# Token dispatch on one core: output tiles of 16 tokens with 64 KB rows, two buffers, and every third product on ScalarE

## The chip, the core and the metric

The kernel runs on one core of a Trainium2 chip. The metric is the device time of one execution in microseconds (us); lower is better. The tensor engine has nothing to do here. The work is done by the DMA engines, which move data between HBM and the on-chip memory (SBUF), and by VectorE (DVE in the profile) and ScalarE (ACT), which multiply. SyncE (SP) multiplies nothing; it issues DMAs.

## The reference

Every token has 512 values and two weights. The output holds each token twice, once scaled by each weight. The expert indices are an input that the result does not depend on.

```python
batch, seq, hidden, n_experts = 16, 1024, 512, 8
k = 2
x_expanded = x[:, :, np.newaxis, :].repeat(k, axis=2)
weights = expert_weights[..., np.newaxis]
return (x_expanded * weights).astype(np.float32)
```

With 16,384 tokens in float32, 33.6 MB are read and 67.1 MB are written.

## The kernel before

The tokens are cut into eight tiles of 2048. In each tile, a partition (one of 128) holds 16 consecutive tokens. Its part of the input is then one contiguous row of 16 x 512 x 4 bytes, 32 KB, and its part of the output is one contiguous row of 64 KB.

**Loads.** `load(i)` takes one input tile of 4 MB into one of two buffers of `x_pool` (line 76). It is issued on ScalarE's queue, so it stands in program order between ScalarE's products. The first two loads are issued ahead of the loop, and `load(i + 2)` at the end of turn `i` (line 109). The eight small weight loads (line 55, 16 KB each) are issued on SP's queue at the start.

**Products.** A tile needs 32 products: 16 tokens times two weights, each over 128 partitions x 512 values. The product of the first weight (`kk == 0`) runs on VectorE (line 97), that of the second (`kk == 1`) on ScalarE (line 91). The number `c` counts the products over the whole kernel: token number times two, plus `kk`.

**Output tiles.** An output tile holds `TO = 8` tokens, so a row of it is 32 KB per partition, and each tile of tokens fills two. `o_pool` has four such buffers. When the eighth token is done, SP issues the store of 4 MB (line 105). It waits there for both engines' products. There are 16 stores.

**What sets the order.** The three queues (SP, ScalarE, VectorE) run in program order, each on its own. A scheduler places the instructions and adds the waits: a product waits for its input tile, for the weights, and for the store that last used its output buffer; a load waits for the products that last read its input buffer. In the built order of the kernel before, each `load(i + 2)` stands behind the first ScalarE product of tile `i + 1`. Every DMA is spread over the same sixteen DMA engines: 128 rows, eight rows to an engine.

Of the kernel before, what the change touches and what calls it, by code (L numbers as in the profile page):

```python
# [1 line left out]

# [4 lines left out]


@with_exitstack
def kernel(  # L10
    ctx: ExitStack,
    tc: tile.TileContext,
    x: bass.AP,
    expert_indices: bass.AP,
    expert_weights: bass.AP,
    out: bass.AP,
):
    nc = tc.nc

    batch, seq, hidden = x.shape  # L20
    k = expert_weights.shape[-1]
    P = nc.NUM_PARTITIONS
    ntok = batch * seq
    assert ntok % P == 0
    A_TOTAL = ntok // P

    f32 = mybir.dt.float32
    row = k * hidden
    TX = 16
    TO = 8  # L30


    groups = [[16], [16], [16], [16], [16], [16], [16], [16]]
    assert sum(sum(g) for g in groups) == A_TOTAL

    xf = x.rearrange("b s h -> (b s) h")
    of = out.rearrange("b s k h -> (b s) (k h)")
    wf = expert_weights.rearrange("b s k -> (b s) k")

    w_pool = ctx.enter_context(tc.tile_pool(name="w_pool", bufs=1))  # L40
    x_pool = ctx.enter_context(tc.tile_pool(name="x_pool", bufs=2))
    o_pool = ctx.enter_context(tc.tile_pool(name="o_pool", bufs=4))

    w_tile = w_pool.tile([P, A_TOTAL * k], f32)

    def rows(of_all, done, T):
        return of_all[done * P : (done + T) * P, :].rearrange(
            "(p a) n -> p (a n)", a=T
        )

    weights = []
    for group in groups:
        weights.append((sum(n for _, n in weights), sum(group)))
    for at, T in weights:
        nc.sync.dma_start(out=w_tile[:, at * k : (at + T) * k], in_=rows(wf, at, T))

    tiles = []
    done = 0
    for group in groups:
        T = sum(group)  # L60
        a0 = 0
        for n in group:
            tiles.append((done, T, a0, n))
            a0 += n
        done += T

    loaded = []

    def load(i):
        if i >= len(tiles):  # L70
            return
        done, T, a0, n = tiles[i]
        x_tile = x_pool.tile([P, TX * hidden], f32)
        cols = rows(xf, done, T)[:, a0 * hidden : (a0 + n) * hidden]
        for lo, hi in [(0, P)]:
            nc.scalar.dma_start(out=x_tile[lo:hi, : n * hidden], in_=cols[lo:hi, :])  # L76
        loaded.append(x_tile)

    for i in range(2):
        load(i)  # L80
    for i, (done, T, a0, n) in enumerate(tiles):
        x_tile = loaded[i]
        outr = rows(of, done, T)
        for t in range(n):
            if t % TO == 0:
                o_tile = o_pool.tile([P, TO * row], f32)
            for kk in range(k):
                c = (done + a0 + t) * k + kk
                o = t % TO * row + kk * hidden
                if kk == 1:  # L90
                    nc.scalar.mul(  # L91
                        out=o_tile[:, o : o + hidden],
                        in_=x_tile[:, t * hidden : (t + 1) * hidden],
                        mul=w_tile[:, c : c + 1],
                    )
                    continue
                nc.vector.tensor_scalar(  # L97
                    out=o_tile[:, o : o + hidden],
                    in0=x_tile[:, t * hidden : (t + 1) * hidden],
                    scalar1=w_tile[:, c : c + 1],  # L100
                    scalar2=None,
                    op0=mybir.AluOpType.mult,
                )
            if (t + 1) % TO == 0:
                nc.sync.dma_start(
                    out=outr[:, (a0 + t + 1 - TO) * row : (a0 + t + 1) * row],
                    in_=o_tile,
                )
        load(i + 2)

# [1 line left out]
_INS = ['x', 'expert_indices', 'expert_weights']  # L112
_OUTS = [((16, 1024, 2, 512), 'float32')]


# [23 lines left out]
```

## Time and profile before

| | |
|---|---|
| median of 11 runs | 240.22 us (240.01 to 241.35) |
| the profiled execution, its own time | 241.35 us |
| its span, first to last instruction | 239.6 us |
| VectorE busy | 51.9 us, 128 products of 480 ns |
| ScalarE busy | 81.3 us, 128 products of 708 ns and a table load |
| moved by DMA | 100.81 MB, mean 421 GB/s |
| DMA issues | 16 stores of 4096 KB, 8 loads of 4096 KB, 8 weight loads of 16 KB |

The profile shows one execution. A row for a group of instructions gives how often it ran, how long it was busy and how long one took. The mean length of one product is longer than the distance from one to the next, since they overlap at their ends: 16 products take 6.42 us on VectorE and 9.91 us on ScalarE. The row of tenths for DMA says how busy the sixteen engines were in each of 40 equal slices, and the row under it how much they moved. The queue named q1 carries what SP issues, q10 what ScalarE issues. Beside the page, the trace keeps a record for every DMA packet: when it started, how long it took, its size and its queue. One packet here is one row of a DMA.

### The profile page before, as it was taken

How to read it: one execution, taken by the hardware profiler on the slowest of the kernel's cores; microseconds unless marked ns; L12 is line 12 of the kernel's file. 1: busy time of each engine (PE TensorE's matmuls, PEld its weight loads, DVE VectorE, ACT ScalarE, POOL GpSimd, SP SyncE). 2: the span in 40 equal slices, each digit the busy share in tenths (PEclk: the TensorE clock that was granted, in tenths of full speed). 3: DMA queues.
4: the chain of work that ended last, by engine and by line, in shares of the span. 5: the costliest groups of instructions: out<-in, count | busy, mean ns of one | idle time of the engine just before them, and what ended most of it. 6: DMA issues, size and time to landing. Idle time of an engine off the chain costs nothing.

```text
span 239.6 us, 384 instructions
## 1 busy us (share of the span) xinstructions
DVE 51.9 (22%) x128; ACT 81.3 (34%) x129; POOL 0.2 (0%) x4
## 2 busy tenths in 40 slices
DVE  0073820055005005050140502204041235000000
ACT  0179880085306108070160803507043266200000
POOL 0000000000000000000000000000000000000000
DMA  6999999999999999999999999999999999999995
GB/s 265 434 439 365 439 438 438 438 427 438 432 416 438 424 372 432 432 438 438 438 427 427 438 427 427 432 427 432 438 432 438 438 438 438 432 432 432 438 438 224
DMA packets 4610, 100.81 MB, mean 421 GB/s; under 512 B 1536, under 2 KB 1536, under 8 KB 1536
## 3 DMA queue, kind: packets, MB, share of 16 engines
q1 hardware_dynamic: 3456, 67.24, 65.3%
q10 hardware_dynamic: 1152, 33.55, 33.3%
q14 instruction: 2, 0.02, 0.0%
HBM read 33.69 MB, written 67.11 MB: 421 GB/s over the span
## 4 chain that ended last, share of the span: by engine, by line
DMA 60%; another core or an unknown queue 12%; ACT 12%; ACTq 1%; issue 0%
DMA out_dram<-o_tile 40%; DMA x_tile<-in_x_dram 18%; ACT o_tile L91 12%; DMA w_tile<-in_expert_weights_dram 2%; ACTq L76 0%; ACTq L134 0%; ACTq L91 0%
## 5 line engine op out<-in xcount | busy, mean ns | idle before, releaser
L91 ACT ACTIVATE o_tile<-x_tile,w_tile 128x512 f32<-128x512 f32 x128 | 80.0, 708 | 118.3 <-DMA out_dram<-o_tile 96.4
L97 DVE TENSOR_SCALAR o_tile<-x_tile,w_tile 128x512 f32<-128x512 f32 x128 | 51.9, 480 | 151.5 <-DMA out_dram<-o_tile 115.9
L91 ACT ACT_TABLE_LOAD x1 | 1.3, 1283 | 5.4 <-DMA w_tile<-in_expert_weights_dram 5.4
L123 POOL MEMSET const-bfloat16-1.0<- 128x1 bf16 x1 | 0.1, 102 | 0.0
L123 POOL MEMSET const-uint8-127<- 128x1 uint8 x1 | 0.1, 102 | 0.0
L123 POOL MEMSET const-float32-0.0<- 128x1 f32 x1 | 0.1, 99 | 0.2 <-issue 0.2
L123 POOL MEMSET const-float32-1.0<- 128x1 f32 x1 | 0.1, 99 | 0.0
## 6 DMA issues: line engine op xcount, KB each, us to landing
out_dram<-o_tile SPq DMA_DIRECT2D x16, 4096.0 KB, 48.4
x_tile<-in_x_dram ACTq DMA_DIRECT2D x8, 4096.0 KB, 23.1
w_tile<-in_expert_weights_dram SPq DMA_DIRECT2D x8, 16.0 KB, 21.7
```

Source lines behind the costliest of these rows:

```text
L91: nc.scalar.mul(out=o_tile[:, o : o + hidden], in_=x_tile[:, t * hidden : (t + 1) * hidden], mul=w_tile[:, c : c + 1],)
L97: nc.vector.tensor_scalar(out=o_tile[:, o : o + hidden], in0=x_tile[:, t * hidden : (t + 1) * hidden], scalar1=w_tile[:, c : c + 1], scala ...
L123: nc = _bacc.Bacc("TRN2", target_bir_lowering=False, num_devices=1)
```

## The change

An output tile now holds 16 tokens: one per tile of tokens, with rows of 64 KB, in two buffers instead of four of half the size. The memory taken is the same. Tile 0 is stored in two pieces, after 8 and after 16 tokens; each of the other seven is stored by one DMA of 8 MB. The products are split by `c % 3`: where it is 2 the product runs on ScalarE (85 in all), otherwise on VectorE (171).

```diff
-    TO = 8
+    TO = 16
...
-    o_pool = ctx.enter_context(tc.tile_pool(name="o_pool", bufs=4))
+    o_pool = ctx.enter_context(tc.tile_pool(name="o_pool", bufs=2))
...
-                if kk == 1:
+                if c % 3 == 2:
                     nc.scalar.mul(
...
-            if (t + 1) % TO == 0:
+
+            n_out = TO // 2 if i == 0 else TO
+            if (t + 1) % n_out == 0:
+                at = t + 1 - n_out
                 nc.sync.dma_start(
-                    out=outr[:, (a0 + t + 1 - TO) * row : (a0 + t + 1) * row],
-                    in_=o_tile,
+                    out=outr[:, (a0 + at) * row : (a0 + t + 1) * row],
+                    in_=o_tile[:, at % TO * row : (at % TO + n_out) * row],
                 )
```

The order of the built instructions changes with it. SP issues nine stores instead of sixteen. On ScalarE, `load(2)` still stands behind the first product of tile 1, but each later `load(i + 2)` now stands behind the last product of tile `i`, ahead of the first product of tile `i + 1`. A product of tile `i` waits for the whole store of tile `i - 2`; the first products of tile 2 wait for both pieces of tile 0.

## The prediction

> **What bounds the kernel now.** I read the page from the top: first the busy shares of the engines, then the DMA row of the 40 slices and the queues, and last who waits for whom.
>
> ```profile
> span 239.6 us, 384 instructions
> DVE 51.9 (22%) x128; ACT 81.3 (34%) x129; POOL 0.2 (0%) x4
> ...
> DMA  6999999999999999999999999999999999999995
> GB/s 265 434 439 365 439 438 438 438 427 438 432 416 438 424 372 432 432 438 438 438 427 427 438 427 427 432 427 432 438 432 438 438 438 438 432 432 432 438 438 224
> ...
> q1 hardware_dynamic: 3456, 67.24, 65.3%
> q10 hardware_dynamic: 1152, 33.55, 33.3%
> ```
>
> No compute engine is busy for more than 34% of the span, and the DMA row is 9 everywhere but in the first and last slice. q1 (stores, and the small weight loads) and q10 (input loads) together take 98.6% of sixteen engines' span. So the sixteen DMA engines are the bound, and only two things can move the time: how long their packets take, and how long they have nothing to do. The stretches say where the missing 1.4% lies (columns: stretch, length, busy us and count of DVE, ACT and POOL, clock, DMA share, GB/s):
>
> ```profile
> 0.00:2.00 2.00, 0.00 (x0) 0.00 (x0) 0.20 (x4) 1.00 0.34 88
> 2.00:20.00 18.00, 6.35 (x16) 7.64 (x12) 0.00 (x0) 1.00 1.00 428
> 20.00:24.00 4.00, 0.07 (x1) 3.55 (x6) 0.00 (x0) 1.00 0.93 283
> 24.00:54.00 30.00, 9.69 (x24) 14.93 (x24) 0.00 (x0) 1.00 1.01 437
> ...
> 84.00:88.00 4.00, 0.00 (x0) 0.00 (x0) 0.00 (x0) 1.00 0.97 336
> 88.00:150.00 62.00, 15.01 (x37) 22.11 (x36) 0.00 (x0) 1.00 1.01 434
> 150.00:210.00 60.00, 14.30 (x36) 22.96 (x37) 0.00 (x0) 1.00 1.00 431
> 210.00:236.00 26.00, 0.00 (x0) 0.00 (x0) 0.00 (x0) 1.00 1.02 439
> ```
>
> Between 24 us and 236 us the rate is 430 to 439 GB/s whether loads and stores mix (24 to 54) or stores run alone (210 to 236), with one dip at 84 to 88. The engines' waits then read differently from what their size suggests:
>
> ```profile
> DVE o_tile L97 <- DMA out_dram<-o_tile: 115.9, 11, 13.8
> ACT o_tile L91 <- DMA out_dram<-o_tile: 96.4, 11, 12.0
> DVE o_tile L97 <- DMA x_tile<-in_x_dram: 35.5, 3, 17.1
> ```
>
> They are slack: VectorE and ScalarE wait for buffers while the DMA engines never stop.
>
> The packet records of the same trace give the budget of one DMA engine. It moves 192 packets of 32 KB (64 of loads, 128 of stores). 2915 of the 3072 last 1213 ns: 192 x 1.213 = 232.9 us. Packets that last longer add 2.1 us per engine: 0.4 in the first 6 us, 0.7 at 20 to 24 us, 0.9 at 83 to 89 us. The 128 B packets of the weights add 0.8 and the 4 B packets that signal completion 0.3. First packet at 1.8 us, last end at 238.4 us, 1.2 us to the end of the span. Idle time of an engine inside 4 to 236 us: none.
>
> **The change part by part.** *Longer rows.* 14 stores of 4 MB become 7 of 8 MB, each with 128 rows of 64 KB; the two pieces of tile 0 keep 32 KB rows. Per engine 7 x 16 = 112 packets of 32 KB become 7 x 8 = 56 of 64 KB. The trace has no 64 KB packet, so I take the line through those that it has: 128 B in 13 ns and 32768 B in 1213 ns give 0.03676 ns per byte and 8.3 ns that do not scale; an 8192 B instruction packet would then take 309.5 ns, and the records show 309. So 64 KB takes 2418 ns against 2 x 1213 = 2426, and the change saves 56 x 8.3 = 0.46 us. Bounds: if a row were moved as two pieces, nothing is saved; on the other side a longer row could run slower per byte for a reason that no packet here shows, and 1% of 2.42 us over 56 packets is 1.36 us. I take 0.46, since three sizes lie on one line.
>
> [...]
>
> *Completion packets.* Seven stores fewer, one 4 B packet of 9 ns each on every engine: 0.06 us. The seven issues of 332 ns that go from SP's queue were behind waits of up to 16 us and save nothing.
>
> *Every third product on ScalarE.* A product takes 6.42 / 16 = 0.401 us on VectorE and 9.91 / 16 = 0.62 us on ScalarE, end to end. Tile by tile it was 16 and 16 (6.4 and 9.9 us); now 21 or 22 on VectorE (8.8 us) and 10 or 11 on ScalarE (6.8 us). A whole tile is ready 1.1 us sooner. Nothing waits for that, except perhaps the first store: its 16 products were 8 x 0.62 = 5.0 us after 13.65 and are 11 x 0.401 = 4.4 us now, so it is issued near 18.1 instead of 18.68. The second load's packets occupy the engines until about 23 us either way. Zero.
>
> *Two buffers of 16 tokens.* A product of tile i may now start only when the whole store of tile i-2 has landed (for tile 2: both pieces), where half of it was enough. Behind that wait stands all of tile i, and SP's store of it. The cover is the store of tile i-1, already queued: 8 x 2.418 = 19.3 us if it has the engines to itself, 29.0 us with a load between its packets. Under it must go the landing (1.2 us or so from the end of the span), 8.8 us of products, 0.35 us of issue and 1.1 us to the first packet (0.72 to 1.8 us at the start): 11.4 us. Slack 7.9 us at the least, near the end, where no load runs. Early on it is larger still: tile 1 is ready at 24.83 + 21 x 0.401 = 33.3 us, and the two pieces of tile 0 keep the engines busy to 23.1 + 19.4 = 42.5 us or longer. Zero.
>
> *The two pieces of tile 0.* Piece one is queued about 5 us before the second load's packets end, piece two near 22.5 us. One whole 16-token store would be queued at 22.5 and start at 23.6, just behind the end of the loads; the split keeps that gap closed. Zero against before, which also stored 8 tokens first.
>
> *Loads that move on ScalarE's queue.* Before, load i+2 for i of 1 and more stood behind the first product of tile i+1, which waited for a buffer: load 3 was issued at 48.45 us, load 4 at 73.78. The built order of the changed kernel puts it right behind tile i's products, so load 3 goes out when VectorE has finished tile 1, near 33.3 us. ScalarE ends tile 1 near 24.83 + 11 x 0.62 = 31.7 and waits 1.6 us there, ahead only of products that wait for stores until after 50 us. Loads then queue behind one another with no pause between them. With packets taken in turn, a load gets a third of the time while 64 KB stores run: 8 x (1.213 + 2.418) = 29.0 us, the same as the work of one tile, and it has about two such periods from issue to use.
>
> [...] The records show turns of one row: from 136 to 152 us 96 store and 114 load packets start, in every 2 us some of each. [...]
>
> **Sum.** -0.46 - 0.06 = -0.52 us. The profiled execution of before took 241.35 us (span 239.6, 1.75 around it), so its like would take 240.83. It is among the slowest of the eleven runs; their median is 240.22, and the 0.9 us dip at 84 to 88 us is about what sets it apart. Against the median: 239.70 us.
>
> **The rivals.** *Nothing saved* (0.10): the 64 KB row is moved in two pieces, or its fixed part overlaps its neighbour. Only the completion packets are left: 240.16. For it: nobody sees the fixed part outside of packet lengths. Against it: packets follow each other without idle time, so length is cost.
>
> *The long row is dearer* (0.13), the case that ends slower. The place is every packet of the seven large stores; it decides at 2.426 us a packet, above which the change loses. At +24 ns (1%) it costs 1.34 us, less 0.06: 241.5; at half that, 240.85. For it: nothing of this size has run here. Against it: 8 KB and 32 KB cost the same per byte.
>
> *The store queue runs dry* (0.03): the wait for a whole 16-token buffer takes the place of the one for half. It decides where 11.4 us of landing, products and issue exceed the 19.3 us of the store before; each us above that costs 1 us in each of up to six tiles. If the products had a fifth more time it would still not happen. 242 if it did.
>
> *The dip goes too* (0.04): the slow read packets at 84 to 88 us (2.5 us for the longest) belong to where a load stood. Loads now stand elsewhere; if the median run has 0.6 us of it, the time is 239.1.
>
> **How the numbers follow.** 0.2% is 0.48 us, about what a measurement of this kernel can tell from no change. The main case (0.70) lies at 239.70, its own range 239.2 to 240.1; about 0.54 of it falls beyond 0.48 us and 0.16 within, for the fixed part may be 4.7 ns. Faster: 0.54 + 0.04 = 0.58. Same: 0.16 + 0.10 = 0.26. Slower: 0.13 + 0.03 = 0.16. The range from 239.0 to 241.0 takes in the main case, nothing saved, and the dearer row up to about 0.6%.
>
> **What would show it.** Right: q1 with 56 x 16 + 7 x 16 = 1008 packets fewer, 2448; the share of the two queues still above 98%; stretches from 24 to 236 us at 430 to 439 GB/s; load 3 issued at about 33 us and load 4 at about 63 (16 store and 9 load packets from 23.1 us, landing near 54, and 8.8 of products); VectorE waiting for stores about once a tile, longer each time. Wrong: 64 KB packets longer than 2.426 us (GB/s under 430 while stores run alone), a slice below 9 in the DMA row between the first and the last, VectorE waiting while the DMA share falls, or q1 at some 3344 packets (rows in two pieces).

## The result, and the profile after

The changed kernel takes 244.0 us (median of 13 runs, 240.83 to 245.93) against 240.13 us for the kernel before (50 runs, 239.81 to 241.45). It is slower: the ratio is 1.0087, with a 95% interval from 1.0065 to 1.0110. The ratio, worth 2.1 us, lies below that of the medians (1.016, or 3.9 us) because it leaves out runs more than 1.5% above the fastest of the same kernel, and the changed kernel has four of them. The runs of the changed kernel are spread over 5 us; those of the kernel before stay within 1.7.

The profile is of an execution of 245.2 us, 1.2 us above the median, so it shows more of the loss than a typical run; the second profile of this kernel (246.09 us, below) does too, and no execution of it near 241 us was profiled. First the page, to be held against the same rows of before: span, busy time, the DMA rows in 40 slices, the queues, and the DMA issues (name, queue, count, KB each, median us to landing).

```profile
span 243.3 us, 364 instructions
DVE 68.4 (28%) x171; ACT 54.2 (22%) x86; POOL 0.2 (0%) x4
...
DMA  6999999999999999998999999999999998989891
GB/s 267 433 433 355 431 431 431 431 436 512 389 463 399 442 404 458 409 475 377 463 420 409 474 366 409 393 431 480 409 420 469 393 496 366 496 366 506 356 431 43
...
q1 hardware_dynamic: 2448, 67.24, 64.3%
q10 hardware_dynamic: 1152, 33.55, 33.1%
...
x_tile<-in_x_dram ACTq DMA_DIRECT2D x8, 4096.0 KB, 34.3
out_dram<-o_tile SPq DMA_DIRECT2D x2, 4096.0 KB, 28.7
...
out_dram<-o_tile SPq DMA_DIRECT2D x7, 51.7
```

q1 holds 2448 packets, so each 64 KB row is one packet. The two queues fill 97.4% of the longer span. Four slices before the last show an 8 in the DMA row, but no engine idles there: the page counts a packet in the slice where it starts, and packets are now twice as long. Summed from the start and end of each packet, the sixteen engines are busy all the time in these four slices, and from 4 to 236 us but for 0.5 us in all of single engines at 146 to 173 us. (A slice's GB/s swings more than before for the same reason.) The issues of loads 3 and 4 (start, length, queue), first before, then after, and what VectorE waited for after (us in total, times, longest):

```profile
48.45 0.33 ACTq L76 DMA_DIRECT2D x_tile<-in_x_dram  x1
73.78 0.33 ACTq L76 DMA_DIRECT2D x_tile<-in_x_dram  x1
```
```profile
32.31 0.36 ACTq L76 DMA_DIRECT2D x_tile<-in_x_dram  x1
67.91 0.36 ACTq L76 DMA_DIRECT2D x_tile<-in_x_dram  x1
...
DVE o_tile L97 <- DMA out_dram<-o_tile: 128.9, 6, 27.2
DVE o_tile L97 <- DMA x_tile<-in_x_dram: 15.0, 2, 13.2
```

The stretches say where the time is (stretch, length, busy us and count of DVE, ACT and POOL, clock, DMA share, GB/s; a packet counts where it starts):

```profile
54.00:76.00 22.00, 8.40 (x21) 6.84 (x11) 0.00 (x0) 1.00 1.02 441
76.00:84.00 8.00, 0.00 (x0) 0.00 (x0) 0.00 (x0) 1.00 1.02 438
84.00:88.00 4.00, 0.00 (x0) 0.00 (x0) 0.00 (x0) 1.00 0.91 377
88.00:150.00 62.00, 17.20 (x43) 13.08 (x21) 0.00 (x0) 1.00 1.00 423
...
236.00:238.00 2.00, 0.00 (x0) 0.00 (x0) 0.00 (x0) 1.00 0.68 295
238.00:240.00 2.00, 0.00 (x0) 0.00 (x0) 0.00 (x0) 1.00 0.23 98
240.00:242.00 2.00, 0.00 (x0) 0.00 (x0) 0.00 (x0) 1.00 0.00 0
```

Two things are new. From 88 to 150 us the rate is 423 GB/s instead of 434 (62 x 11 / 434 = 1.6 us), though the DMA engines are busy but for 0.4 us of single ones. And the end is long: a share of 0.23 in two microseconds is 7.4 engine-microseconds, three packets of 2.418 us. Three engines work on after the other thirteen have finished.

The records of the packets show who they are. A record doesn't name its engine, but each packet starts within a few ns of the end of the one before it on its engine, so the records join into sixteen chains of 136 large packets each. "Stretched" is the time by which large packets last longer than 8.3 ns + 0.03676 ns per byte, as a mean over the engines.

| kernel profiled | last packet of each engine ends at (us) | stretched, us per engine |
|---|---|---|
| before | 236.8 to 238.4 | 2.1 |
| before, a second execution (240.2 us) | 236.2 to 237.2 | 1.5 |
| changed | seven at 236.6 to 237.0, six at 238.8 to 239.3, three at 241.4 to 242.1 | 3.55 |

Every engine has the same 72 store and 64 load packets. Where packets of several engines end together, a chain can be joined in more than one way; the ends and the mean don't depend on that, the sum of one chain does. With this reserve, the early ones lost about 2 us in stretched packets, most of it in the first 30 us as before, and the last about 6 to 7. The last end sets the span: 242.1 + 1.2 = 243.3 us. Nine in ten of the 64 KB packets take 2418 ns to the nanosecond, and the stretched ones up to 3033.

### The profile page after: what moved, and what is told of

It is laid out like the page before. It is cut to its first block, busy times and chain, and to the rows that moved or that the text cites. A ratio compares the mean times of both kernels' runs of the same rounds, so it can differ in the third digit from the quotient of the medians.

```text
span 243.3 us, 364 instructions
## 1 busy us (share of the span) xinstructions
DVE 68.4 (28%) x171; ACT 54.2 (22%) x86; POOL 0.2 (0%) x4
## 3 DMA queue, kind: packets, MB, share of 16 engines
q1 hardware_dynamic: 2448, 67.24, 64.3%
## 4 chain that ended last, share of the span: by engine, by line
DMA 58%; another core or an unknown queue 15%; DVE 11%; ACT 2%; issue 1%; DVEq 0%; SPq 0%; ACTq 0%
DMA x_tile<-in_x_dram 37%; DMA out_dram<-o_tile 18%; DVE o_tile L97 11%; DMA w_tile<-in_expert_weights_dram 2%; ACT o_tile L91 2%; DVEq L137 0%; DVEq L97 0%; SPq L108 0%; ACTq L76 0%
## 5 line engine op out<-in xcount | busy, mean ns | idle before, releaser
L97 DVE TENSOR_SCALAR o_tile<-x_tile,w_tile 128x512 f32<-128x512 f32 x171 | 68.4, 480 | 143.9 <-DMA out_dram<-o_tile 128.9
L91 ACT ACTIVATE o_tile<-x_tile,w_tile 128x512 f32<-128x512 f32 x85 | 52.9, 708 | 150.3 <-DMA out_dram<-o_tile 140.2
```

The costliest lines, as they stand in the source:

```text
L91: nc.scalar.mul(out=o_tile[:, o : o + hidden], in_=x_tile[:, t * hidden : (t + 1) * hidden], mul=w_tile[:, c : c + 1],)
L97: nc.vector.tensor_scalar(out=o_tile[:, o : o + hidden], in0=x_tile[:, t * hidden : (t + 1) * hidden], scalar1=w_tile[:, c : c + 1], scala ...
```

## The experiments

Two theories stood at first. Theory 1: 64 KB packets, while loads share the engines, make single engines lose time. Theory 2: the two whole-tile buffers, and the loads that leave a tile earlier, cost the time.

**32 KB rows in the changed kernel** (rows32, and again beside the changed kernel).

```diff
-                nc.sync.dma_start(
-                    out=outr[:, (a0 + at) * row : (a0 + t + 1) * row],
-                    in_=o_tile[:, at % TO * row : (at % TO + n_out) * row],
-                )
+                for lo in range(at, t + 1, TO // 2):
+                    nc.sync.dma_start(
+                        out=outr[:, (a0 + lo) * row : (a0 + lo + TO // 2) * row],
+                        in_=o_tile[:, lo % TO * row : (lo % TO + TO // 2) * row],
+                    )
```

> The changed kernel, but each of the seven whole tiles is stored by two DMAs with 32 KB rows, issued one behind the other when the tile is done. Buffers, products, waits and the place of the loads are those of the changed kernel. Theory 1 (the 64 KB packet, while loads share the engines, makes single engines lose time): back to 240.0 to 240.5 us, engines ending within 2 us of each other. Theory 2 (two whole-tile buffers and loads issued a tile earlier): stays at 243 to 245 us with a ragged end of some 5 us.

> The changed kernel once more, beside its variant with 32 KB rows on the same chip: 241 to 246 us again, median near 244, engines ending in groups some 2.4 us (one 64 KB packet) apart.

> The changed kernel with its whole tiles stored by two DMAs with 32 KB rows, once more: if the row length carries part of the loss, its median lies 1 to 2.5 us under that of the changed kernel of the same chip, and its engines end within 2 us. If the earlier loads and the two buffers carry all of it, the two agree within 0.5 us.

Measured: 242.22 us (241.59 to 243.78; before 240.71 on that chip), ratio 1.0069 (1.0042 to 1.0096). On a second chip, side by side: the changed kernel 242.47 us (240.22 to 246.74), with 32 KB rows 242.69 us (241.14 to 243.36), before 240.25. Theory 1 falls as it stood: with 32 KB rows the kernel stays 1.5 to 2.4 us above the kernel before, and the two medians of one chip agree (ratios 1.0042, 1.0005 to 1.0080, and 1.0072, 1.0037 to 1.0107). But they are slow in different ways. With 32 KB rows the engines end within 1.8 us of each other and the runs within 2.2; with 64 KB the chains end 6.4 us apart in the second profile (246.09 us) and the runs 6.5. With 32 KB rows stretched time is 2.96 us per engine, against 1.5 in the second profile of the kernel before, and it falls on all engines at once, for example between 170 and 180 us (stretches of its second run):

```profile
121.00:170.00 49.00, 13.82 (x35) 10.70 (x18) 0.00 (x0) 1.00 1.00 431
170.00:180.00 10.00, 0.40 (x2) 0.56 (x1) 0.00 (x0) 1.00 1.00 390
180.00:236.00 56.00, 16.80 (x43) 12.52 (x21) 0.00 (x0) 1.00 1.01 434
```

In these 10 us fifteen engines have a stretched packet in the same row of the same load (450 ns in the mean), and then in the next row (528 ns). So there are two losses to explain.

**Loads held back in the changed kernel** (load_late). An extra product of one column reads the old input buffer, so the load into it can leave only when the next tile has its output buffer.

```diff
                 o_tile = o_pool.tile([P, TO * row], f32)
+                if 2 <= i < len(tiles) - 1:
+                    nc.scalar.mul(
+                        out=o_tile[:, 0:1], in_=loaded[i - 1][:, 0:1], mul=w_tile[:, 0:1]
+                    )
```

> The changed kernel with 64 KB rows, but load i+2 is held until tile i+1 has its output buffer, as in the kernel before: one extra product of a single column per tile reads the old input buffer first. Theory 2 (early loads, queued behind one another) expects 240 to 241 us. Theory 1 expects the loss to stay: 242 to 245 us, since loads still share the engines with 64 KB stores.

**The changed kernel with every second product on ScalarE** (even_split).

```diff
-                if c % 3 == 2:
+                if kk == 1:
```

> The changed kernel with the products split as before (every second on ScalarE). Both theories: as the changed kernel, 242 to 245 us, spread over several us from run to run. If the split has a part in the loss, it falls below 242.

Measured: 245.94 us (242.97 to 249.79) and 244.65 us (239.92 to 250.14), against 240.71. Neither is a clean test. In load_late each held load also stood behind the next tile's first product on ScalarE, which waits for that tile's own input. So from load 4 on each left only when the one before had landed (load 7 at 189.70 us), VectorE waits seven times for an input, and the DMA engines run dry. In even_split the order moved too: load 3 stood behind the first product of tile 2 again and left at 53.56 us. Loads 5 to 7 were issued within 1 us of their times in the changed kernel, but stood in the queue behind load 3; loads 3 to 7 landed 14 to 17 us later than there, and some engines had nothing to do at 217 to 219 us (a DMA share of 0.77 from 216 to 220). Waits (who, for what, us in total, times, longest) and a stretch of load_late:

```profile
DVE o_tile L101 <- DMA x_tile<-in_x_dram: 129.1, 7, 26.1
ACT o_tile L88 <- DMA out_dram<-o_tile: 79.0, 5, 23.5
...
186.00:192.00 6.00, 2.26 (x6) 2.36 (x4) 0.00 (x0) 1.00 0.80 311
```

A share of 0.80 over 6 us is the dry stretch: eleven of its chains have a gap, most of about 2 us, at 190.7, while the other five, which had lost 6 to 8 us in stretched packets, still work. What these two do show is that 64 KB rows with loads as late as these are no way out. Loads held only to the times of the kernel before were not tried with 64 KB rows. The best run of even_split, 239.92 us, is the lowest of any run with 64 KB rows and all loads.

**The split alone, in the kernel before** (third_only, and again), **and with its loads held** (third_late, and again).

```diff
-                if kk == 1:
+                if c % 3 == 2:
```
```diff
                 o_tile = o_pool.tile([P, TO * row], f32)
+                if t == 0 and 1 <= i < len(tiles) - 1:
+                    nc.scalar.mul(
+                        out=o_tile[:, 0:1], in_=loaded[i - 1][:, 0:1], mul=w_tile[:, 0:1]
+                    )
```

> The kernel before with nothing but the split changed (every third product on ScalarE). Theories 1 and 2: 240.1 us, no change, since nothing waits for products. If the loss comes from the split: 241 or more.

> The kernel before with every third product on ScalarE, and with each load held until the next tile has its first output buffer (one extra product of one column per tile reads the old input buffer), so that loads leave when they leave in the kernel before. If the 1.05 us of the split alone came from the earlier loads: back within 0.3 us of the kernel before. If it came from the products themselves: stays 0.6 to 1.5 us above it.

> The kernel before with every third product on ScalarE, beside its variant with held loads on the same chip. If loads that leave 6 to 10 us earlier cost about 1 us: 241.2 to 242 us. If the earlier value was the chip's: 240.2 to 240.6 us.

> The kernel before with every third product on ScalarE and each load held until the next tile has its first output buffer. If the time of the loads matters: 240.2 to 240.6 us, 0.7 to 1.5 us under the variant whose loads leave early. If not: the same as that variant within 0.3 us.

Measured: 241.76 us alone (before 240.71) and 240.51 with held loads (before 240.22); then on one chip 241.57 us alone (241.06 to 242.68; ratio 1.0058, 1.0036 to 1.0080) and 240.53 with held loads (240.26 to 242.09; ratio 1.0018, 1.0002 to 1.0035), before 240.23. The split by itself costs 1.3 us, and 1.0 of it goes when the loads leave where they left before. The issues of the last four loads, from the two timelines of that chip (start, length, queue), first of the split alone, then with held loads:

```profile
73.12 0.34 ACTq L76 DMA_DIRECT2D x_tile<-in_x_dram  x1
93.28 0.36 ACTq L76 DMA_DIRECT2D x_tile<-in_x_dram  x1
125.96 0.35 ACTq L76 DMA_DIRECT2D x_tile<-in_x_dram  x1
154.63 0.35 ACTq L76 DMA_DIRECT2D x_tile<-in_x_dram  x1
```
```profile
73.27 0.33 ACTq L76 DMA_DIRECT2D x_tile<-in_x_dram  x1
102.28 0.33 ACTq L76 DMA_DIRECT2D x_tile<-in_x_dram  x1
131.49 0.33 ACTq L76 DMA_DIRECT2D x_tile<-in_x_dram  x1
160.48 0.33 ACTq L76 DMA_DIRECT2D x_tile<-in_x_dram  x1
```

In neither do the DMA engines run dry. What differs is when the loads run: three of them leave 5.5 to 9 us sooner and so meet other store rows. Stretched time is 1.97 us per engine with the early loads and 1.42 with the held ones. In the early kernel, twelve engines have a stretched packet in one row of load 7, at 160 us, and its engines end at 236.5 to 238.6 us, against 236.1 to 237.2 for the held one. That the faster products move the loads at all is the scheduler's doing: in the built order those loads stand ahead of the next tile's first product on ScalarE. 0.3 us remains with held loads, and what makes it is not settled.

**Loads on SP's queue** (one_queue64).

```diff
-            nc.scalar.dma_start(out=x_tile[lo:hi, : n * hidden], in_=cols[lo:hi, :])
+            eng = nc.scalar if i < 2 else nc.sync
+            eng.dma_start(out=x_tile[lo:hi, : n * hidden], in_=cols[lo:hi, :])
```

> The changed kernel with loads 2 to 7 issued on SP's queue, each right behind the store of the tile two before it, so that on every DMA engine loads and 64 KB stores follow one another and their packets never take turns. Theory 1 (the loss comes from loads and 64 KB stores taking turns on an engine): 239.5 to 240.2 us and engines that end within 2 us of each other. Rival 1b (a 64 KB store costs time by itself, through anything but its packet's length): stays at 242 to 245 us.

**Stores alone, with 64 KB and with 32 KB rows** (noload64, noload32).

```diff
-        x_tile = loaded[i]
+        x_tile = loaded[i % 2]
...
-        load(i + 2)
```

> The changed kernel with loads 2 to 7 left out (tiles 2 to 7 use the first two input tiles again, so the output differs): only stores from about 23 us on. Theory 1: no stretched packets after 30 us; per engine 16 load and 16 store packets of 1.213 and 56 of 2.418 us, 174.2 us, and about 7 us around them: 181 to 182 us, the same within 0.3 us in every run, engines ending within 2 us. Rival 1b: 2 to 4 us more, and spread from run to run.

> Loads 2 to 7 left out as in the run of stores alone, so the output differs, but with 32 KB rows for the whole tiles: 56 packets of 64 KB become 112 of 32 KB. By the packet count 0.46 us for the packets and 0.06 for completions: 182.56 us against 182.04. If the fixed part of a packet costs no time, 182.0.

Measured: stores alone 182.04 us with 64 KB rows (181.86 to 182.29) and 182.37 with 32 KB (182.28 to 182.54). The difference is 0.33 us where 0.52 was expected. It comes from four runs each on two chips; a 95% interval worked out from these eight runs goes from about 0.1 to 0.6 us, so there is a saving, and its size is not settled. Each kernel's runs lie within 0.5 us. No 64 KB packet in that profile takes longer than 2768 ns, the 99th in a hundred takes 2441, and the engines end at 177.9 to 179.1 us. So the long packet is not dear by itself; the loss was there only with loads. One queue took 242.44 us (241.17 to 243.82, ratio 1.0094, 1.0058 to 1.0129): my theory expected 240. Loads 2 to 7 and the stores are on one queue here (q1 moved 92.41 MB, q10 8.39). In the packet records of this run the two kinds no longer take turns on an engine, and eleven engines end at 236.2 to 237.0 us, but five end between 237.5 and 239.3. In the same records their stretched packets are mostly the last rows of a load, which ran while engines that were ahead had gone over to the store. So taking turns on one engine isn't needed for the loss. That some engines load while others store fits these records, but no run isolates it.

**16 KB store rows in the kernel before** (store16), **and 16 KB rows for both** (both16). Packets are of unequal length here too, but none is long.

```diff
-                nc.sync.dma_start(
-                    out=outr[:, (a0 + t + 1 - TO) * row : (a0 + t + 1) * row],
-                    in_=o_tile,
-                )
+                for lo in range(t + 1 - TO, t + 1, TO // 2):
+                    nc.sync.dma_start(
+                        out=outr[:, (a0 + lo) * row : (a0 + lo + TO // 2) * row],
+                        in_=o_tile[:, lo % TO * row : (lo % TO + TO // 2) * row],
+                    )
```
```diff
-        x_tile = x_pool.tile([P, TX * hidden], f32)
+        x_tile = x_pool.tile([P, TX * hidden + 8], f32)
...
+        half = n // 2 * hidden
+        nc.scalar.dma_start(
+            out=x_tile[:, :].rearrange("p (h m) -> p h m", h=2)[:, :, :half],
+            in_=cols.rearrange("p (h m) -> p h m", h=2),
+        )
```

> The kernel before with each store cut into two DMAs with 16 KB rows. 128 packets more per engine at 8.3 ns and 16 completion packets at 9 ns: 1.2 us more by packet count alone, 241.4 us. If packets of unequal length on the two queues are enough to set the engines out of step, it costs more: 242.5 to 245 us, spread from run to run, as with 64 KB. If it takes the 64 KB packet itself, 241.2 to 241.7 us in nearly every run.

> The variant of the kernel before with 16 KB store rows, with its loads cut to 16 KB rows as well (one DMA per tile still, two rows per partition), so that packets on both queues are equal again and half as long as before. By packet count it is dearer than with 16 KB stores alone: 64 more load packets at 9 ns, 0.6 us. Theory 1c (unequal packet lengths on two queues set the engines out of step, and out of step they stretch each other's packets): falls from 245.9 to 241.5 to 242.5 us, engines ending within 2 us. If more packets or more DMAs in flight are what costs: 246 us or more.

Measured: 245.87 us with 16 KB stores and 32 KB loads (245.75 to 246.65; ratio 1.0227, 1.0191 to 1.0263); 242.37 us with 16 KB for both (242.25 to 242.75; ratio 1.0090, 1.0076 to 1.0104). The order of instructions on every queue is the same, and the second has 64 packets more per engine, yet it is 3.5 us faster, each beside a kernel before of 240.2 us. Stretched time is 3.8 us per engine in store16 and 1.8 in both16. The time of both16 is nearly what its packets cost: 128 + 64 more at about 9 ns (a 16 KB packet takes 611 ns, two 1222 against 1213), 1.7 us, and 0.14 for completions, on 240.23, make 242.07. The two ends, first store16, then both16:

```profile
236.00:238.00 2.00, 0.00 (x0) 0.00 (x0) 0.00 (x0) 1.00 1.01 434
238.00:240.00 2.00, 0.00 (x0) 0.00 (x0) 0.00 (x0) 1.00 0.37 156
240.00:242.00 2.00, 0.00 (x0) 0.00 (x0) 0.00 (x0) 1.00 0.31 131
```
```profile
236.00:238.00 2.00, 0.00 (x0) 0.00 (x0) 0.00 (x0) 1.00 0.80 344
238.00:240.50 2.50, 0.00 (x0) 0.00 (x0) 0.00 (x0) 1.00 0.05 16
```

With unequal rows ten engines end by 238.6 us and six between 240.9 and 243.2; with equal rows all end between 237.5 and 238.8. So a ragged end needs no 64 KB packet; rows of unequal length on the two queues brought it here. By which way is open, for the place of the loads changes too: load 3 is issued at 43.99 us in store16 and at 49.08 in both16, load 7 at 164.95 and 161.17, and a load beside stores takes 14 to 17 us from first row to last with unequal rows, 19 to 20 with equal ones.

**The kernel before again, and two variants meant to be faster** (before_again, one_w, w_first). Each of the two loads all weights in one DMA, one_w on SP's queue, w_first on ScalarE's ahead of the inputs.

```diff
-    for at, T in weights:
-        nc.sync.dma_start(out=w_tile[:, at * k : (at + T) * k], in_=rows(wf, at, T))
+    T = groups[0][0]
+    nc.scalar.dma_start(
+        out=w_tile.rearrange("p (g n) -> p g n", n=T * k),
+        in_=wf.rearrange("(g p a) k -> p g (a k)", p=P, a=T),
+    )
```

> The kernel before once more, as a kernel of its own: ratio 1.000 within 0.3%. Its profile shows whether the stretched load packets at 84 to 88 us are there in every execution. Theory 1 expects stretched packets to be few and shared by all engines, so that the engines end within 2 us.

> The kernel before with its eight weight loads made one DMA (the same 1024 rows of 128 B). In the records each engine's last load packet of tile 1 is stretched at 20 to 24 us, 0.7 to 0.9 us per engine, while the weight rows of the last weight load, issued only when tile 0 had landed, run between. If those rows cause it: 239.3 to 239.6 us. If not: 240.1 us, no change.

> The kernel before with its weights in one DMA issued on ScalarE's queue ahead of the first input load, so that no weight row stands between load rows. Its 64 rows per engine cost the same 0.8 us, and the input of tile 0 lands about as before. If the weight rows between load rows stretch the last load packets (0.7 to 0.9 us per engine at 20 to 24 us in every kernel), it gains that: 239.2 to 239.7 us, faster than both kernels. If the stretch belongs to the change from loads to stores there: 240.0 to 240.3 us.

Measured: 240.18 us for the kernel before (ratio 0.9993, 0.9977 to 1.0009); 249.22 for one_w (248.90 to 249.57); 241.65 for w_first (240.89 to 242.94; ratio 1.0043, 1.0019 to 1.0066). In the second profile of the kernel before, only three load packets and two store packets after 28 us are stretched by over 60 ns: the dip at 84 to 88 us is not there in every execution. one_w is slower because the products wait for the weights:

```profile
DVE o_tile L100 <- DMA w_tile<-in_expert_weights_dram: 23.9, 1, 23.9
ACT L94 <- DMA w_tile<-in_expert_weights_dram: 23.8, 1, 23.8
```

An engine has 64 weight rows of 128 B and 16 load rows of 32 KB, and the rows go about one for one while both are queued (in the kernel before, 228 weight rows and 234 load rows start from 2 to 20 us): the weights landed when the loads were through, at 23.8 us, and the DMA engines then stood still for about 8 us. w_first did nearly take away the stretched packets at 20 to 24 us (0.11 us per engine instead of 0.7 or more). That doesn't show that weight rows make them: in one_w, too, weight rows run between the load rows and behind the last of them (567 of the 1024 at 20 to 24 us), and no load packet there is stretched. What stretches them in the kernel before is open. In w_first others came at 36 to 40 us (0.56) and one engine ended 2.4 us after the rest. No version here that makes all the loads beats the kernel before.

## Why the prediction was wrong, point by point

**Right: the bound and the packet.** The DMA engines stayed the bound. The 64 KB row is one packet of 2418 ns, as the line through 128 B, 8 KB and 32 KB said, and q1 lost exactly 1008 packets. The rival that the long row is dearer in itself falls, and so does the one that nothing is saved: stores alone were 0.33 us faster with it. The chances also allowed for a fixed part of 4.7 ns a packet; no run shows that figure. What the runs showed in its place is the 2418 ns of the 64 KB packet, which agrees with the 8.3 ns of the trace's line, and the 0.33 us, whose interval of 0.1 to 0.6 takes in the 0.52 of the sum but is too wide to fix the price of a packet.

**The signs.** Three signs named ahead went the wrong way: the share of the two queues (97.4%, above 98% was forecast), the rates between 24 and 236 us (377 to 441 GB/s instead of 430 to 439), and slices below 9. The last one misleads, since the engines are busy there. No sign named the end of each engine, and that is where the time showed.

**Small slips.** The dearer row at half of 1% comes to 240.22 + 0.67 - 0.06 = 240.83 us, not 240.85. The longest packet at 84 to 88 us lasted 2.65 us, not 2.5. And in the profile of before, the product ahead of load 3 waited for its input, not for a buffer (that of load 4 did wait for a buffer). None of them changes the forecast.

**Right: the waits.** Load 3 left at 32.31 us and load 4 at 67.91 (I had 33 and 63), VectorE waited for stores six times, up to 27.2 us, and the DMA engines did not run dry in the changed kernel. Store 1 and later ones were queued in time. The rival of the dry queue was not this kernel's loss. DMA engines did run dry in load_late and even_split, but there because loads came late.

**Wrong: the step "loads that move on ScalarE's queue", costed at nothing.** Its working asked only whether a load arrives in time. It does. But where a load lay against the stores changed how long packets took: 1.97 us of stretched time per engine in third_only and 1.42 in third_late, whose times are 1.0 us apart and whose queues differ in little else. The claim beside it, that the split is worth zero, fails with it: alone in the kernel before it cost 1.3 us, 1.0 of it through the loads that it moved. In the changed kernel the split is not what moves most loads: in even_split loads 5 to 7 are issued at nearly the same times. That the moved loads cost the changed kernel its time is carried over from this pair; the attempt to hold them there (load_late) was no clean test.

**Wrong: "packets taken in turn", as a matter of who gets which share.** I took the 2.1 us of stretched packets as fixed and counted sixteen engines as one. With a 2.418 us packet on one queue and 1.213 on the other, the engines ended in groups (from 236.6, 238.8 and 241.4 us on), and the slowest engine set the end. My reading is that groups out of step stretch each other's packets, some loading while others store; that is argued, not shown. The sum had no term for it. In the profiled execution that term was 1.4 us in the mean (stretched time rose from 2.1 to 3.55 us) and 3.7 us for the last engine (242.1 instead of 238.4), seven times the saving of 0.52 us that was forecast. The pair store16 and both16 shows the dependence on unequal length without any long packet, with 3.5 us between them.

**The dip.** The rival that it goes because loads stand elsewhere falls. In the kernel before it is there in one of two profiles; in the changed kernel packets like these come at each of the store boundaries at 86, 115, 143 and 172 us (0.3, 0.3, 1.0 and 0.4 us per engine around them).

What remains open: why a packet is stretched while other engines do the opposite. The records give when and by how much, not which memory or path is at fault. On the one chip where both ran side by side, 64 KB and 32 KB rows had the same median, so how the loss of the changed kernel divides between early loads and unequal rows is not settled; each was shown in a kernel of its own. Nor was the third part of the change ever tried alone: the two buffers of 16 tokens, which let a tile start only when a whole store has landed. No DMA engine ran dry because of them, but they too set when loads and stores run.

## What to carry to other kernels

When the DMA engines are the bound, count each of them: here the first had its last packet behind it at 236.6 us and the last at 242.1, which set the end and which the mean rate hid, so look at the last slices and at where each engine's last packet ends. Try rows of one length for loads and stores that run together: halving both cost 2.1 us here beyond the kernel before, halving one cost 5.6. It is no cure for all, for in the changed kernel rows of one length left the median where it was (242.69 against 242.47 us). And treat an edit to the products as an edit to the loads wherever a load stands in an engine's program order: compare the load issue times before giving it a cost of nothing (here loads that left 5.5 to 9 us sooner cost 1.0 us).

## What was not expected of the hardware

The DMA engines, with the same rows to move, ended 5.5 us apart in the profile of the changed kernel (236.6 to 242.1), in groups about one 64 KB packet (2.4 us) apart. A load packet of 32 KB that takes 1213 ns lasted up to 2824 in the changed kernel, with no more than 0.5 us of single engines idle from 4 to 236 us. A queue of 128 B rows beside one of 32 KB rows got about one row for each of the other's (228 and 234 from 2 to 20 us in the kernel before), and in one_w 128 KB of weights took 23.0 us to land.
